# The first two dense units on x transposed by the host, the norm put into weights and results, and h made meanwhile

## The chip, the cores and the metric

The kernel runs on one core of a Trainium2 chip. The metric is device time in microseconds; the time before is 746.34 us, the median of three runs (745.83 to 747.23). Names of engines: PE is TensorE, DVE is VectorE, ACT is ScalarE, POOL is GpSimd, SP is SyncE, which issues nearly all DMAs here.

## What is computed

One decoder block on x, 256 tokens by 1024 channels, fp32. What matters for the change is its start:

```python
h = rmsnorm(x, g_mix[l])
proj = h @ w_in[l]
q_d, k_d, v_d, q_s, k_s, v_s, gate_d, gate_s = split_cols(proj, IN_WIDTHS)
```

with

```python
y = x32 * lax.rsqrt(jnp.mean(x32 * x32, axis=-1, keepdims=True) + RMS_EPS)
return (y * gain.astype(jnp.float32)).astype(x.dtype)
```

So h[t, c] = x[t, c] * r[t] * g[c], with one factor r per token and one gain g per channel. Behind it come dilated attention in three groups and sliding-window attention, two branch products merged by sigmoid gates, an output product added to x, a second norm (gain g_ffn), a router and 32 experts, of which each token uses two, and a final norm.

## The kernel before

Partitions are 128 wide, so D = 1024 is NK = 8 slices of channels and T = 256 tokens are NT = 2 tiles. The dense projection is cut into units of 512 output columns (`units`, in the order q, k, v of dilated group 1, then of groups 2 and 0, then the others). A unit's weights are two loads of 1 MB (`Stream.load`, L172, on SP; the very first load is split in two). Each fp32 operand is split into an upper part rounded to fp32r and a lower part, the remainder; `three` (L354) adds three products: upper by upper, lower by upper, upper by lower. `convert` (L240) makes both parts of two slices of a unit's weights: ACT casts the upper part (L257), DVE subtracts for the lower one (L258). There are four such pairs of buffers (set_split in the trace), so a unit's four conversions wait until TensorE has left the ones before.

`unit_steps` (L452) runs a unit in two passes of half its columns, four steps of two slices each, and `evac` (L370) takes a result out of PSUM. For q and k units the weights are stationary and h transposed (`hT_hi`, `hT_lo`, set_hT in the trace) moves, 256 columns an instruction; for v units hT is stationary and the weights move, 512 columns. Results go to two PSUM banks in turn (`acc`, L348). Four more banks (`quad`) serve the attention later.

At the start x is loaded with tokens on partitions (L148, L150). ACT and DVE each square half of a tile and sum it (L298, L299), a square root and a reciprocal give r (L285, L286), and `diag` is the identity times r (L307). A product of a slice of x with diag (`turn`, L310) then transposes it and puts r on it at once. The gain, brought to columns by a small transposing product (L303), goes on as the slice is read out of PSUM: ACT makes hT_hi (L319), DVE hT_lo (L320). Between them the first unit's weights are converted.

The order on each engine is made by a scheduler from the program's order and its dependences; `pin` keeps an instruction in the program's order. After the attention the tiles of finished stages are handed to a ring (`release`, L678), into which SP loads the expert weights (`prefetch`, L687), 2 MB a piece, 96 pieces.

Of the kernel before, what the change touches and what calls it, by code (L numbers as in the profile page):

```python
# [17 lines left out]
P = 128  # L18
T = 256
# [65 lines left out]
def tile_hybrid_block(  # L85
    ctx: ExitStack,
    tc: tile.TileContext,
    x, g_mix, w_in, w_kvs, sinks, w_br_dil, w_br_swa, w_out, g_ffn, w_group, b_group,
# [54 lines left out]
    xt = lay(4, "x", 0, [P, NT, D])  # L143
    cs = sb.tile([P, C_SMALL], F32, tag="cs", name="cs")
    ident = cs[:, C_ID:C_ID + P]
    grow = sb.tile([8, P], F32, tag="ct1", name="grow")
    frow = sb.tile([8, P], F32, tag="ct0", name="frow")
    SP.dma_start(xt[:, 0, :], x[0:P])  # L148
    A.dma_start(ident, c_small[:, C_ID:C_ID + P])
    SP.dma_start(xt[:, 1, :], x[P:T])  # L150
    A.dma_start(grow, g_mix[0].rearrange("(k p) -> k p", p=P))
# [13 lines left out]
    class Stream:  # L165
# [6 lines left out]
        def load(self):  # L172
# [41 lines left out]
    SP.dma_start(cs[:, P:], c_small[:, P:])  # L214
    SP.dma_start(frow, g_ffn[0].rearrange("(k c) -> k c", c=P))
# [24 lines left out]
    def convert(order=lambda i: i):  # L240
# [6 lines left out]
        while stream.n <= n:  # L247
# [9 lines left out]
        order(A.copy(w[:, 0, :, :ncol], r))  # L257
        order(V.tensor_tensor(  # L258
            out=w[:, 1, :, :ncol], in0=r, in1=w[:, 0, :, :ncol].bitcast(F32), op=ALU.subtract))
# [54 lines left out]
    for k in range(7):  # L314
        turn(k)
# [136 lines left out]
    def unit_steps(u):  # L452
# [5 lines left out]
        for half in range(npass):  # L458
            acc.n += 1
            o = acc()  # L460
            for kp in range(nkp):
# [26 lines left out]
                if kp == nkp - 1:  # L488
                    evac(un, half, o)
# [705 lines left out]
```

## Time and profile before

| | |
|---|---|
| time, median of three runs | 746.34 us (745.83 to 747.23) |
| the profiled execution, its own time | 747.22 us |
| its span | 745.3 us |
| TensorE busy | 627.6 us, 84% of the span |
| DVE, ACT, POOL busy | 295.3, 224.7 and 2.1 us |
| share of the chain that ended last | DMA 47%, PE 27%, ACT 5%, DVE 5% |
| expert weights on that chain | 36% and 11% of the span |

The share of busy time is a mean over stages with different limits. The chain is followed back from the last instruction to what released it each time, so it tells which engine or transfer was late in each stage; the busy times of a stretch tell how full an engine is there.

### The profile page before, as it was taken

What the parts mean: (1) busy time and instruction counts of PE and PEld (TensorE: products, weight loads), DVE (VectorE), ACT (ScalarE), POOL (GpSimd) and SP (SyncE); (2) the same over time, 40 slices, a digit from 0 to 9 for tenths busy, and PEclk for the clock granted to TensorE, in tenths of its full rate; (3) what the DMA queues carried; (4) which work ended last, traced back from release to release, by engine and by line L of the source; (5) the groups of instructions that cost most, each with busy time, mean ns of one, the idle gap of its engine ahead of it and who ended that gap; (6) DMA issues with size and microseconds to landing.
All of it is one profiled execution on the core that took longest, in us unless ns stands there. A gap on an engine that the chain in (4) does not pass through costs nothing.

```text
span 745.3 us, 14687 instructions
## 1 busy us (share of the span) xinstructions
PE 627.6 (84%) x6416; PEld 462.6 (62%) x6416; DVE 295.3 (40%) x753; ACT 224.7 (30%) x450; POOL 2.1 (0%) x10
## 2 busy tenths in 40 slices
PE   9999999999999999999887767776877677668773
PEld 8999988888998998655555434443533353334341
DVE  6554767985788566432222111211211121111003
ACT  6444566775788443301111001000100010000004
POOL 0000000000000000000000000000000000000000
PEclk9999999999999999999999878997878997997796
DMA  8746446337537978999999999999999999999992
GB/s 324 271 186 226 142 142 226 115 114 239 214 114 306 377 284 309 368 430 425 426 426 428 425 426 426 426 427 425 429 424 430 423 427 428 426 426 427 426 394 99
DMA packets 25940, 249.86 MB, mean 335 GB/s; under 512 B 5120, under 2 KB 6544, under 8 KB 8336
## 3 DMA queue, kind: packets, MB, share of 16 engines
q1 hardware_dynamic: 25712, 248.81, 82.1%
q8 instruction: 52, 0.85, 0.5%
q14 instruction: 16, 0.13, 0.0%
q10 hardware_dynamic: 160, 0.07, 0.0%
HBM read 247.82 MB, written 1.05 MB: 334 GB/s over the span
## 4 chain that ended last, share of the span: by engine, by line
DMA 47%; PE 27%; ACT 5%; DVE 5%; issue 1%; SPq 0%; DVEq 0%
DMA ew<-in_w_e_gu_dram 36%; PE acc L132 12%; DMA ew<-in_w_e_down_dram 11%; PE gu L132 5%; PE quad L132 2%; PE ga L132 2%; PE dn L132 2%; DVE set_split L258 2%; ACT set_probs L514 1%; DVE set_probs L525 1%; PE dpv L132 1%; PE dtp L594 1%; ACT set_split L257 1%; DVE set_qs L410 1%; DVE set_probs L512 1%
## 5 line engine op out<-in xcount | busy, mean ns | idle before, releaser
L132 PE MATMUL gu<-ew,xes 128*32 128x256 f32 x2048 | 152.2, 431 | 44.3 <-DMA ew<-in_w_e_gu_dram 44.2
L132 PE MATMUL acc<-set_hT,set_split 128*128 128x256 f32 x1200 | 151.6, 282 | 0.8 <-DVE set_qa L410 0.8
L132 PEld LDWEIGHTS acc<-set_hT,set_split 128*128 128x128 f32 x1200 | 142.5, 189 | 2.5 <-DVE set_qa L410 1.0
L132 PEld LDWEIGHTS gu<-ew,xes 128*32 128x32 f32 x2048 | 67.4, 120 | 106.3 <-DMA ew<-in_w_e_gu_dram 56.7
L258 DVE TENSOR_TENSOR set_split<-set_raw,set_split 128x1024 fp32r<-128x1024 f32 (+1 forms) x84 | 100.2, 1198 | 33.6 <-ACT set_split L257 31.2
L257 ACT CAST set_split<-set_raw 128x1024 fp32r<-128x1024 f32 (+1 forms) x84 | 86.3, 1028 | 41.8 <-PE acc L132 41.0
L966 DVE TENSOR_TENSOR set_raw<-set_raw,gu 128x128 f32<-128x128 f32 x32 | 9.2, 287 | 201.9 <-ACT set_raw L963 201.9
L963 ACT ACTIVATE set_raw<-gu 128x128 f32<-128x128 f32 x32 | 8.9, 277 | 230.3 <-PE gu L132 230.3
L132 PE MATMUL dn<-ew,set_raw 128*32 128x256 f32 x1024 | 71.7, 423 | 7.1 <-DMA ew<-in_w_e_down_dram 6.6
L132 PEld LDWEIGHTS dn<-ew,set_raw 128*32 128x32 f32 x1024 | 34.0, 119 | 30.8 <-issue 6.5
L132 PE MATMUL ga<-set_raw 128*128 128x128 f32 x256 | 39.5, 318 | 5.0 <-DVE set_raw L979 4.2
L992 ACT ACTIVATE y_hi<-dn,gsl 128x256 fp32r<-128x256 f32 x32 | 15.1, 473 | 91.0 <-PE dn L132 91.0
L132 PEld LDWEIGHTS ga<-set_raw 128*128 128x128 f32 x256 | 36.1, 226 | 8.9 <-DVE set_raw L979 7.0
L994 DVE SCALAR_TENSOR_TENSOR y_lo<-dn,gsl,y_hi 128x256 fp32r<-128x256 f32 x32 | 15.4, 480 | 53.5 <-ACT y_hi L992 53.5
L132 PE MATMUL acc<-set_split,set_hT 128*128 128x512 f32 x144 | 34.1, 394 | 0.3 <-DVE set_ks L420 0.2
L891 ACT ACTIVATE xes<-ga,fcol 128x128 f32<-128x128 f32 x32 | 11.6, 367 | 69.5 <-DVE xes L893 69.5
L933 DVE TENSOR_SCALAR set_raw<-cs,pos 128x128 f32<-128x128 f32 x64 | 17.8, 282 | 37.0 <-PE ct L132 37.0
L132 PE MATMUL quad<-y_hi,cts 32*128 32x256 f32 x256 | 23.7, 349 | 8.5 <-ACT y_hi L992 8.5
L132 PEld LDWEIGHTS acc<-set_split,set_hT 128*128 128x128 f32 x144 | 26.7, 188 | 6.6 <-DVE set_split L258 0.6
L132 PE MATMUL quad<-y_lo,cts 32*128 32x256 f32 x256 | 21.9, 347 | 7.7 <-DVE y_lo L994 6.5
L138 PE MATMUL atp<-cs,set_raw 128*128 128x128 f32 x32 | 11.5, 360 | 19.0 <-DVE set_raw L966 18.2
L138 PEld LDWEIGHTS atp<-cs,set_raw 128*128 128x128 f32 x32 | 4.7, 148 | 36.3 <-DVE set_raw L966 33.8
(205 smaller groups left out, 644.7 us busy)
## 6 DMA issues: line engine op xcount, KB each, us to landing
ew<-in_w_e_gu_dram SPq DMA_DIRECT2D x62, 2048.0 KB, 39.1
ew<-in_w_e_down_dram SPq DMA_DIRECT2D x31, 2048.0 KB, 39.1
set_raw<-in_w_in_dram SPq DMA_DIRECT2D x29, 1024.0 KB, 5.0
set_raw<-in_w_br_swa_dram SPq DMA_DIRECT2D x4, 1024.0 KB, 5.0
set_raw<-in_w_out_dram SPq DMA_DIRECT2D x4, 1024.0 KB, 6.2
ew<-in_w_e_gu_dram SPq DMA_DIRECT2D x4, 1024.0 KB, 33.1
set_raw<-in_w_br_dil_dram SPq DMA_DIRECT2D x2, 1024.0 KB, 4.9
set_x<-in_x_dram SPq DMA_DIRECT2D x2, 512.0 KB, 4.7
```

Source lines behind the costliest of these rows:

```text
L132: i = PE.matmul(o, lhsT, rhs, start=start, stop=stop, skip_group_check=True)
L138: i = PE.transpose(o, src, ident)
L257: order(A.copy(w[:, 0, :, :ncol], r))
L258: order(V.tensor_tensor(out=w[:, 1, :, :ncol], in0=r, in1=w[:, 0, :, :ncol].bitcast(F32), op=ALU.subtract))
L410: V.scalar_tensor_tensor(out=lo, in0=sv, scalar=cs[own, j:j + 1], in1=hi.bitcast(F32), op0=ALU.mult, op1=ALU.subtract)
L512: V.tensor_tensor_reduce(out=v, in0=s, in1=dist, scale=float(scale), scalar=init, op0=ALU.add, op1=ALU.min, accum_out=nm[:, i:i + 1])
L891: A.activation(dst, src, AF.Copy, scale=col)
L933: eq = V.tensor_scalar(dd[:, t, :].rearrange("p (g s) -> p g s", g=REP), cs[:, C_CNT:C_CNT + CAP].unsqueeze(1).to_broadcast([P, REP, CAP]) ...
L963: A.activation(ac, gu[:, 0:P], AF.Silu)
L966: V.tensor_tensor(out=ac, in0=ac, in1=gu[:, P:2 * P], op=ALU.mult)
L992: A.activation(y_hi, dn[:, 0:256], AF.Copy, scale=gsl)
L994: V.scalar_tensor_tensor(out=y_lo, in0=dn[:, 0:256], scalar=gsl, in1=y_hi.bitcast(F32), op0=ALU.mult, op1=ALU.subtract)
```

## The change

The host gives x transposed (`xT`: channels on partitions, slice by slice) beside x, and both gains as one small array of columns (`gcols`, on ACT's queue). The kernel loads the first four slices of xT, then the first half-piece of weights, then the other four slices, then the rest as before. The table of constants comes in one load.

For the first two units (q and k of group 1) the moving operand is x itself, `xT_hi` cast by ACT and `xT_lo` subtracted by POOL. Their weights get the gain as they are converted, in instructions of one slice each: ACT scales by the gain's column, DVE multiplies by it and subtracts. Their results stay in the four quad banks (`put_off`) until r is there, and get r as they are read out (`rbc`, r on all partitions, one column per token).

r comes from squares of xT (half on DVE, half on POOL), added by POOL, reduced over slices by DVE (`hsum`), summed over partitions by a product with a matrix of ones, then a square root on ACT and a reciprocal on DVE (`scale_rows`). h for the other units is made in `normal`, four times for two slices: POOL multiplies xT by rbc, ACT multiplies by the gain's columns and casts hT_hi, POOL subtracts for hT_lo. The sum of squares by ACT and DVE on tokens, diag, the transposing products and both small transposes of gains are gone.

```diff
-    xt = lay(4, "x", 0, [P, NT, D])
+    xt = lay(4, "x", 0, [P, NK, T])
     cs = sb.tile([P, C_SMALL], F32, tag="cs", name="cs")
     ident = cs[:, C_ID:C_ID + P]
-    grow = sb.tile([8, P], F32, tag="ct1", name="grow")
-    frow = sb.tile([8, P], F32, tag="ct0", name="frow")
-    SP.dma_start(xt[:, 0, :], x[0:P])
-    A.dma_start(ident, c_small[:, C_ID:C_ID + P])
-    SP.dma_start(xt[:, 1, :], x[P:T])
-    A.dma_start(grow, g_mix[0].rearrange("(k p) -> k p", p=P))
+    gcols = sb.tile([P, 2 * NK], F32, tag="gcols", name="gcols")
+    gcol, fcol = gcols[:, 0:NK], gcols[:, NK:]
+    A.dma_start(gcols, gains_in)
+    SP.dma_start(xt[:, 0:4, :], xT[:, 0:4, :])
...
                 SP.dma_start(t[:, j:j + step, :ncol], src[:, j:j + step, :])
+                if self.n == 0 and j == 0:
+                    SP.dma_start(xt[:, 4:, :], xT[:, 4:, :])
             self.tiles[self.n] = (t, s)
...
         stream.load()
-    SP.dma_start(cs[:, P:], c_small[:, P:])
-    SP.dma_start(frow, g_ffn[0].rearrange("(k c) -> k c", c=P))
+    SP.dma_start(cs, c_small)
...
         r = raw[:, 2 * half:2 * half + nk, :ncol]
-        order(A.copy(w[:, 0, :, :ncol], r))
-        order(V.tensor_tensor(
-            out=w[:, 1, :, :ncol], in0=r, in1=w[:, 0, :, :ncol].bitcast(F32), op=ALU.subtract))
+        if u < 2:
+            for j in range(nk):
+                col = gcol[:, 2 * kp + j:2 * kp + j + 1]
+                order(A.activation(w[:, 0, j, :], r[:, j, :], AF.Copy, scale=col))
+                order(V.scalar_tensor_tensor(out=w[:, 1, j, :], in0=r[:, j, :], scalar=col,
+                                             in1=w[:, 0, j, :].bitcast(F32), op0=ALU.mult, op1=ALU.subtract))
+        else:
+            order(A.copy(w[:, 0, :, :ncol], r))
+            order(V.tensor_tensor(
+                out=w[:, 1, :, :ncol], in0=r, in1=w[:, 0, :, :ncol].bitcast(F32), op=ALU.subtract))
         wtiles[(u, kp)] = w
...
-    ht = lay(4, "x", 2048, [P, NT, D])
-    ssq = sm("ssq", [P, 2, 2])
-    rs0 = sm("rs0", [P, 2])
-    diag = sb.tile([P, 1024], F32, tag="PT", name="diag")
+    G = nc.gpsimd
+    sq = lay(4, "x", 2048, [P, NK, T])
     hT_hi = lay(0, "hT", 0, [P, NK, T], F32R)
     hT_lo = lay(0, "hT", 2048, [P, NK, T], F32R)
+    xT_hi = lay(1, "xT", 0, [P, NK, T], F32R)
+    xT_lo = lay(1, "xT", 2048, [P, NK, T], F32R)
+    rbc = sb.tile([P, T], F32, tag="yh", name="rbc")
     pin = tc.keep_in_program_order
-    gcol = sm("gcol", [P, 8])
-    fcol = sm("fcol", [P, NK])
-    for t in range(NT):
-        pin(A.activation(ht[:, t, 0:512], xt[:, t, 0:512], AF.Square, accum_out=ssq[:, t, 0:1]))
-        pin(V.tensor_tensor_reduce(out=ht[:, t, 512:D], in0=xt[:, t, 512:D], in1=xt[:, t, 512:D], scale=1.0,
-                                   scalar=0.0, op0=ALU.mult, op1=ALU.add, accum_out=ssq[:, t, 1:2]))
-        if t == 1:
-            gps = bank("A1", [P, 512], "gps")
-            PE.transpose(gps[:, 0:8], grow, ident[0:8, 0:8])
-            pin(V.tensor_copy(gcol, gps[:, 0:8]))
-        pin(V.tensor_tensor(out=ssq[:, t, 0:1], in0=ssq[:, t, 0:1], in1=ssq[:, t, 1:2], op=ALU.add))
-        rstd_of(rs0[:, t:t + 1], ssq[:, t, 0:1])
-        pin(V.tensor_scalar(diag[:, t * P:(t + 1) * P], ident, rs0[:, t:t + 1], None, op0=ALU.mult))
-    hps = [bank(b, [P, 512], f"hps{b}")[:, 0:T] for b in ("T", "V", "A0")] + [quad[k][:, 0:T] for k in range(4)]
-    def turn(k):
-        for t in range(NT):
-            mm(hps[k][:, t * P:(t + 1) * P], xt[:, t, k * P:(k + 1) * P], diag[:, t * P:(t + 1) * P], True, True)
-    for k in range(7):
-        turn(k)
+    pin(V.tensor_tensor(out=sq[:, 0:4, :], in0=xt[:, 0:4, :], in1=xt[:, 0:4, :], op=ALU.mult))
     for kq in range(4):
+        if kq % 2 == 0:
+            for k0 in ((0, 2) if kq == 0 else (4,)):
+                k = slice(k0, 4 if kq == 0 and k0 else k0 + (2 if kq == 0 else 4))
+                pin(A.copy(xT_hi[:, k, :], xt[:, k, :]))
+        k = slice(2 * kq, 2 * kq + 2)
+        pin(G.tensor_tensor(out=xT_lo[:, k, :], in0=xt[:, k, :], in1=xT_hi[:, k, :].bitcast(F32), op=ALU.subtract))
         convert(pin)
-        for k in (2 * kq, 2 * kq + 1):
-            pin(A.activation(hT_hi[:, k, :], hps[k], AF.Copy, scale=gcol[:, k:k + 1]))
-            pin(V.scalar_tensor_tensor(
-                out=hT_lo[:, k, :], in0=hps[k], scalar=gcol[:, k:k + 1],
-                in1=hT_hi[:, k, :].bitcast(F32), op0=ALU.mult, op1=ALU.subtract))
-            if k == 0:
-                hps.append(bank("T", [P, 512], "hps7")[:, 0:T])
-                turn(7)
-    fps = bank("T", [P, 512], "fps")
-    PE.transpose(fps[:, 0:8], frow, ident[0:8, 0:8])
-    V.tensor_copy(fcol, fps[:, 0:8])
+    pin(G.tensor_tensor(out=sq[:, 4:, :], in0=xt[:, 4:, :], in1=xt[:, 4:, :], op=ALU.mult))
+    pin(G.tensor_tensor(out=sq[:, 0:4, :], in0=sq[:, 0:4, :], in1=sq[:, 4:, :], op=ALU.add))
+    hsum = sb.tile([P, T], F32, tag="yl", name="hsum")
+    def scale_rows():
+        pin(V.tensor_reduce(hsum, sq[:, 0:4, :].rearrange("p k t -> p t k"), axis=AX.X, op=ALU.add))
+        hs = bank("T", [P, 512], "hs")[:, 0:T]
+        i = PE.matmul(hs, warm[:, 0:1].to_broadcast([P, P]), hsum, start=True, stop=True, skip_group_check=True)
+        pin(A.activation(rbc, hs, AF.Sqrt, scale=1.0 / D, bias=eps))
+        pin(V.reciprocal(rbc, rbc))
+    def normal(kq):
+        k = slice(2 * kq, 2 * kq + 2)
+        G.tensor_tensor(out=sq[:, k, :], in0=xt[:, k, :], in1=rbc.unsqueeze(1).to_broadcast([P, 2, T]), op=ALU.mult)
+        for i in (2 * kq, 2 * kq + 1):
+            A.activation(sq[:, i, :], sq[:, i, :], AF.Copy, scale=gcol[:, i:i + 1])
+        A.copy(hT_hi[:, k, :], sq[:, k, :])
+        G.tensor_tensor(out=hT_lo[:, k, :], in0=sq[:, k, :], in1=hT_hi[:, k, :].bitcast(F32), op=ALU.subtract)
...
                 if kind == "qd" and arg:
-                    V.tensor_scalar(qk[arg][:, 0, c, :], src, cs[:, C_QD + c:C_QD + c + 1], None, op0=ALU.mult)
+                    q, sc = qk[arg][:, 0, c, :], cs[:, C_QD + c:C_QD + c + 1]
+                    if un is units[0]:
+                        V.scalar_tensor_tensor(out=q, in0=src, scalar=sc, in1=rbc, op0=ALU.mult, op1=ALU.mult)
+                    else:
+                        V.tensor_scalar(q, src, sc, None, op0=ALU.mult)
                     continue
...
         elif kind == "kd":
-            A.copy(qk[arg][:, 1, 2 * half:2 * half + 2, :], ov)
+            ks = qk[arg][:, 1, 2 * half:2 * half + 2, :]
+            if un is units[1]:
+                V.tensor_tensor(out=ks, in0=ov, in1=rbc.unsqueeze(1).to_broadcast([P, 2, T]), op=ALU.mult)
+            else:
+                A.copy(ks, ov)
         elif kind == "vd" and arg == 0:
...
             acc.n += 1
-            o = acc()
+            o = quad[2 * u + half] if u < 2 else acc()
             for kp in range(nkp):
...
                     else:
-                        b_hi, b_lo = hT_hi, hT_lo
+                        b_hi, b_lo = (xT_hi, xT_lo) if u < 2 else (hT_hi, hT_lo)
                     for cc in range(2):
...
                 if kp == nkp - 1:
-                    evac(un, half, o)
+                    if u < 2:
+                        put_off.append(lambda half=half, o=o: evac(un, half, o))
+                    else:
+                        evac(un, half, o)
                 if half == npass - 1:
...
-    for _ in steps_of(("qd", "kd", "vd")):
+    first = steps_of(("qd", "kd", "vd"))
+    for i in range(24):
+        next(first)
+        if i == 6:
+            scale_rows()
+        if 8 <= i < 16 and i % 2 == 0:
+            normal(i // 2 - 4)
+        if i >= 18 and put_off:
+            put_off.pop(0)()
+    for _ in first:
         pass
...
     a["x"] = a["x"].reshape(n // 4, 4, d).transpose(1, 0, 2).reshape(1, n, d)
+    a["xT"] = a["x"][0].T.reshape(NK, P, n).transpose(1, 0, 2)
+    a["gains"] = np.concatenate([a[g][0].reshape(NK, P).T for g in ("g_mix", "g_ffn")], axis=1)
     w = a["w_in"][0]
```

What stands on the engines' queues. Names are those of the program; `set_split` are the converted weights, `set_raw` the loaded ones, `set_x` holds x and the squares, `set_xT` the two parts of x, `set_hT` those of h. The lines of the changed kernel have its own numbers.

POOL, from the start to the first instruction that was there before as well; before:

```order
L154 MEMSET warm 128x1
L155 MEMSET warm 128x1
L898 ISA
L898 TENSOR_SCALAR set_raw_87<-cs,pos,rs_194 128x32 x4
L1029 TENSOR_LOAD overi
```

and now:

```order
L152 MEMSET warm 128x1
L153 MEMSET warm 128x1
L311 ISA
L311 TENSOR_TENSOR set_xT<-set_x,set_xT 128x512 x4
L313 TENSOR_TENSOR set_x<-set_x 128x1024
L314 TENSOR_TENSOR set_x<-set_x 128x1024
L328 TENSOR_TENSOR set_x<-set_x,rbc 128x512 x4
L332 TENSOR_TENSOR set_hT<-set_x,set_hT 128x512 x4
L922 TENSOR_SCALAR set_raw_84<-cs,pos,rs_153 128x32 x4
```

Fourteen instructions have come to POOL, ahead of the four of the first gather (L898, now L922).

ACT, from the first unit's weights to the third unit's; before:

```order
L319 ACTIVATE set_hT<-hpsA_135,gcol 128x256
L319 ACTIVATE set_hT<-quad_61,gcol 128x256
L257 CAST set_split_167<-set_raw_90 128x1024
L319 ACTIVATE set_hT<-quad_62,gcol 128x256
L319 ACTIVATE set_hT<-quad_63,gcol 128x256
L257 CAST set_split_167<-set_raw_90 128x1024
L319 ACTIVATE set_hT<-quad_64,gcol 128x256
L319 ACTIVATE set_hT<-hps_155,gcol 128x256
L257 CAST set_split_150<-set_raw_87 128x1024 x2
L257 CAST set_split_167<-set_raw_90 128x1024 x2
L423 COPY set_qk<-acc_311 128x512
L257 CAST set_split_150<-set_raw_87 128x1024 x2
```

and now:

```order
L259 ACTIVATE set_split_129<-set_raw_88,gcols 128x512 x4
L322 ACTIVATE rbc<-hs,warm 128x256
L330 ACTIVATE set_x<-set_x,gcols 128x256 x3
L331 CAST set_hT<-set_x 128x512
L330 ACTIVATE set_x<-set_x,gcols 128x256 x2
L331 CAST set_hT<-set_x 128x512
L330 ACTIVATE set_x<-set_x,gcols 128x256 x2
L331 CAST set_hT<-set_x 128x512
L263 CAST set_split_116<-set_raw_84 128x1024 x2
L330 ACTIVATE set_x<-set_x,gcols 128x256
L331 CAST set_hT<-set_x 128x512
L263 CAST set_split_129<-set_raw_88 128x1024 x2
```

h stood between the first unit's weights; now it stands behind those of the first two units, and the third unit's first two casts (L263) behind three quarters of it.

DVE, around the reduction of the squares (L319, `hsum`); before there was none, and here stood:

```order
L258 TENSOR_TENSOR set_split_167<-set_raw_90,set_split_167 128x1024
L320 SCALAR_TENSOR_TENSOR set_hT<-quad_64,gcol,set_hT 128x256
L320 SCALAR_TENSOR_TENSOR set_hT<-hps_155,gcol,set_hT 128x256
L258 TENSOR_TENSOR set_split_150<-set_raw_87,set_split_150 128x1024
L397 TENSOR_SCALAR set_qk<-acc_199,cs 128x256 x2
```

and now:

```order
L304 TENSOR_TENSOR set_x<-set_x 128x1024
L260 SCALAR_TENSOR_TENSOR set_split_116<-set_raw_84,gcols,set_split_116 128x512 x4
L260 SCALAR_TENSOR_TENSOR set_split_129<-set_raw_88,gcols,set_split_129 128x512 x4
L260 SCALAR_TENSOR_TENSOR set_split_116<-set_raw_84,gcols,set_split_116 128x512 x4
L260 SCALAR_TENSOR_TENSOR set_split_129<-set_raw_88,gcols,set_split_129 128x512 x2
L319 TENSOR_REDUCE hsum<-set_x 128x256
L544 TENSOR_SCALAR nsink<-sink 128x16
L260 SCALAR_TENSOR_TENSOR set_split_129<-set_raw_88,gcols,set_split_129 128x512 x2
L323 RECIPROCAL rbc<-rbc 128x256
L403 SCALAR_TENSOR_TENSOR set_qk<-quad_61,cs,rbc 128x256 x2
```

The reduction stands behind fourteen of the sixteen weight instructions of the first two units, two more stand between it and the reciprocal, and the reading out of the first unit stands behind both. On TensorE the product with ones stands behind the first unit's 96 products and 20 of the second's.

## Rows read from the trace of the kernel before

**Rows 1.** Chain that ended last, in order of time (start us, us, what).

```profile
356.57 1.43 PE gu L132 x22
...
358.54 39.15 DMA ew<-in_w_e_gu_dram
397.75 40.67 DMA ew<-in_w_e_gu_dram
```

**Rows 2.** Busy us by stretch: length, engines with instructions, granted clock, DMA share, GB/s.

```profile
0.00:10.00 10.00, 8.20 (x38) 6.78 (x39) 3.80 (x13) 5.39 (x13) 0.31 (x6) 1.00 0.79 295
10.00:20.00 10.00, 10.00 (x86) 9.62 (x84) 8.97 (x15) 6.55 (x12) 0.00 (x0) 1.00 0.84 311
...
44.00:100.00 56.00, 55.24 (x433) 53.00 (x432) 33.32 (x38) 28.83 (x37) 0.00 (x0) 1.00 0.50 170
...
300.00:350.00 50.00, 48.49 (x614) 29.44 (x613) 17.08 (x77) 8.49 (x26) 0.00 (x0) 0.97 0.98 407
...
400.00:450.00 50.00, 35.36 (x412) 20.89 (x408) 9.02 (x33) 4.00 (x11) 0.00 (x0) 0.82 1.01 426
```

**Rows 3.** Timeline of TensorE in the first three units (start us, us).

```profile
10.27 0.48 PE L132 MATMUL acc<-set_hT,set_split 128*128 128x256 f32 x2
...
11.22 8.77 PE L132 MATMUL acc<-set_hT,set_split 128*128 128x256 f32 x74
...
20.07 13.42 PE L132 MATMUL acc<-set_hT,set_split 128*128 128x256 f32 x116
33.32 11.15 PE L132 MATMUL acc<-set_split,set_hT 128*128 128x512 f32 x48
```

**Rows 4.** Timeline of ACT: its first instruction on x.

```profile
5.02 0.63 ACT L298 ACTIVATE set_x<-set_x 128x512 f32<-128x512 f32 x1 [1.50 <-DMA set_x<-in_x_dram]
```

**Rows 5.** Timeline of SP's queue, then what two of these issues waited for.

```profile
7.81 0.33 SPq L222 DMA_DIRECT2D set_probs<-c_big_dram  x1
9.10 0.33 SPq L224 DMA_DIRECT2D sink<-in_sinks_dram  x1
11.64 0.38 SPq L229 DMA_DIRECT2D wr<-in_w_group_dram  x1
14.07 0.37 SPq L230 DMA_DIRECT2D wr<-in_w_router_dram  x1
16.59 0.37 SPq L229 DMA_DIRECT2D wr<-in_w_group_dram  x1
...
SPq L224 <- DMA set_raw<-in_w_in_dram: 1.0, 1, 1.0
SPq L222 <- DMA set_raw<-in_w_in_dram: 0.8, 1, 0.8
```

**Rows 6.** Groups of instructions by line and form: count, busy us, mean ns of one.

```profile
L257 ACT CAST set_split<-set_raw 128x1024 fp32r<-128x1024 f32 x80 | 83.8, 1049 | 38.4 <-PE acc L132 37.7 <-ACT set_qa L418 0.3 <-ACT set_yd L610 0.2
L257 ACT CAST set_split<-set_raw 128x512 fp32r<-128x512 f32 x4 | 2.5, 620 | 3.4 <-PE acc L132 3.4
L298 ACT ACTIVATE set_x<-set_x 128x512 f32<-128x512 f32 x2 | 1.3, 630 | 1.5 <-DMA set_x<-in_x_dram 1.5
L319 ACT ACTIVATE set_hT<-quad,gcol 128x256 fp32r<-128x256 f32 x4 | 1.8, 488 | 0.0
L258 DVE TENSOR_TENSOR set_split<-set_raw,set_split 128x1024 fp32r<-128x1024 f32 x80 | 97.4, 1224 | 29.4 <-ACT set_split L257 27.0
L258 DVE TENSOR_TENSOR set_split<-set_raw,set_split 128x512 fp32r<-128x512 f32 x4 | 2.8, 693 | 4.3 <-ACT set_split L257 4.3
L132 PE MATMUL spun<-set_probs 128*128 128x256 f32 x12 | 5.0, 597 | 1.2 <-DVE set_probs L160 1.2
```

**Rows 7.** The same view: POOL's only tensor work, and small DVE instructions.

```profile
L898 POOL TENSOR_SCALAR set_raw<-cs,pos,rs 128x32 f32<-128x32 f32 x4 | 1.8, 472 | 296.3 <-ACT junk L717 296.3
L523 DVE RECIPROCAL den<-den 128x4 f32<-128x4 f32 x8 | 1.4, 175 | 0.2
L523 DVE RECIPROCAL den<-den 128x2 f32<-128x2 f32 x8 | 1.3, 162 | 1.6 <-ACT set_probs L514 1.6
L761 DVE TENSOR_SCALAR set_raw<-cs,f 128x32 f32<-128x32 f32 x2 | 0.5, 242 | 0.1
```

More of the change, by code (lines that the diff above doesn't have):

```diff
@@ L87, in tile_hybrid_block @@
     tc: tile.TileContext,
-    x, g_mix, w_in, w_kvs, sinks, w_br_dil, w_br_swa, w_out, g_ffn, w_group, b_group,
+    x, xT, gains_in, w_in, w_kvs, sinks, w_br_dil, w_br_swa, w_out, w_group, b_group,
     w_router, b_router, w_e_gu, w_e_down, g_final, c_small, c_big, out,
@@ L357, in three @@
         mm(o, a_hi, b_lo, False, stop)
-    freed = []
+    freed, put_off = [], []
     flip = [0]
@@ L1141, in tile_hybrid_block @@
     general(*tiles)
-_INS = ["x", "g_mix", "w_in", "w_kvs", "sinks", "w_br_dil", "w_br_swa", "w_out", "g_ffn", "w_group", "b_group",
+_INS = ["x", "xT", "gains", "w_in", "w_kvs", "sinks", "w_br_dil", "w_br_swa", "w_out", "w_group", "b_group",
         "w_router", "b_router", "w_e_gu", "w_e_down", "g_final"]
```

## The prediction

> **What bounds the kernel now.** I read the chain that ended last first, then the busy time by stage, then the first 45 us of TensorE's timeline, then the transfers and the single durations. In the last half the expert weights bound it: from 358.54 us on the chain is one DMA of expert weights after another [rows 1]. Just ahead of that it runs through TensorE [rows 1], which is 97% busy from 300 to 350 us while the DMA is at 0.98 [rows 2]. That DMA stream refills tiles as the earlier stages let go of them, so it is neither earlier nor later than they are. From 10 to 20 us TensorE is busy all the time and from 44 to 100 us 99%, at the full granted clock of 1.00 [rows 2]. I therefore take it that a microsecond won or lost in the first three dense units goes through to the end one for one.
>
> In that front TensorE starts on acc at 10.27, is gapless from 11.22, and begins the third unit at 33.32 [rows 3]. 116 matmuls of 256 columns take 13.42 us, 0.1157 us each; 48 of 512 columns take 11.15, 0.232 each; so the third unit ends at 33.32 + 11.15 = 44.47 [rows 3]. **44.47 is the mark**: what the change makes of it is what it makes of the time.
>
> **What is removed.** The squares, the two diag multiplications, the sixteen transposing products and eight hT_hi/hT_lo pairs leave the front. What this can give: x is there at 5.02 [rows 4]. SP's issues that wait for the weight pieces show them landing about 7.8, 9.1, 11.6, 14.1 and 16.6 us, 1.3 us for 512 KB [rows 5]. The changed queue puts the first half-piece of weights second, so it lands at 6.5, and the second half of x at 7.8; the rest is unchanged. A scaled 128x512 ACT instruction costs 0.63 [rows 6], so TensorE begins at about 7.1. The next half-piece comes at 9.1, its scaled form at 9.7; TensorE has used up its first 24 matmuls (2.8 us) by then. From 9.7 the other 168 take 19.4 us, and the one product for the sum of squares some 0.5 (an estimate; the fp32 warm-up's rows have 597 ns [rows 6]): units one and two could end at 29.6 instead of 33.3. If the third followed at once, the mark would be 40.8, **3.7 us earlier**. That is the ceiling of the gain.
>
> ACT's sixteen scaled instructions at 0.63 replace eight casts at 1.05, 1.7 us more; DVE's sixteen of 128x512 at 0.69 replace eight at 1.22, 1.3 us more [rows 6]. The landings leave both room, so I cost this at nothing. The smaller loads on ACT's queue and the whole constant table in one piece change a few KB: nothing.
>
> **What is added: h, on a path through GpSimd.** Every product of the third unit needs h, and GpSimd's queue now holds, in this order, four 128x512 lower halves of x, two 128x1024 instructions for the sum of squares, four 128x512 multiplications and four 128x512 lower halves of h. GpSimd's price is not in this trace: its only tensor rows are four 128x32 ones at 472 ns, against 242 for a TENSOR_SCALAR of the same size on DVE, 1.95 times as long [rows 7]. *Lower bound*: GpSimd's fixed part (472 less 32 columns at DVE's 1.04 ns, 0.44 us) plus 512 columns at DVE's rate, 0.97 us. *Upper bound*: the row scaled by columns, 7.5 us, which is absurd, since the row is nearly all fixed part. I take twice DVE's duration, a = 1.39 us for 512 columns and b = 2.45 for 1024. The Trainium skill (GPSIMD Engine Reference, Performance versus the Vector engine) gives 4497 ns for a tensor_tensor of 2048 fp32 columns, an estimate of 1.12 for 512; by it the four multiplications below would take 1.1 us less and the undisturbed sum would be -2.0. No run here shows it yet.
>
> The path, if GpSimd and DVE do not disturb one another: ACT scales two weight pieces and casts the second half of x, 9.1 + 2 x 0.63 + 1.05 = 11.4. GpSimd's two remaining lower halves, the squares and the addition, 2a + 2b = 7.7, end at 19.1. The reduction stands on DVE behind fourteen of the sixteen weight instructions, whose pieces land up to 16.6 and whose tiles unit one must release: about 19.8, so the addition is just hidden. Reduction 1.2 (as a 1024-column instruction) gives 21.0; product 0.5 and square root 0.5 give 22.0. The reciprocal goes by (175 - 162)/2 = 6.5 ns a column [rows 7], 1.8 us for 256; with two weight instructions ahead of it on DVE, 24.4. GpSimd's four multiplications, 4a = 5.6, give 30.0. Now **ACT's queue** counts: the third unit's weight casts stand behind the scaling and casting of h. Scaling 0.49 and cast 0.62 give 31.1; two weight casts 33.2; the last quarter of h 34.3; two more casts 36.4; DVE's lower half of the last, 37.6. TensorE still has some 26 matmuls of 512 columns then, 6.0 us: **43.6**, against 44.47. So undisturbed the change is worth only -0.9 us; 2.8 of the 3.7 go into the path of h. Each 0.1 us on a costs nearly 1 us, since 6a + 2b stand on this path.
>
> **The wait that is added.** GpSimd's instructions up to the addition lie beside ten DVE instructions that read two tiles in SBUF, as they do themselves. No row shows such a pair: the four GpSimd rows stand beside DVE work that reads PSUM or a few columns. Bounds: nothing, or each waits while the other reads. For the second, DVE reads 0.53 of its 0.69 us (slope and fixed part of the 512 and 1024 rows [rows 6]), 10 x 0.53 = 5.3; some of this fits into GpSimd's four fixed parts, 4 x 0.44 = 1.8. The addition ends at 11.4 + 7.7 + 5.3 - 1.8 = 22.6 and the reduction begins 2.8 us late. Behind it are queued DVE's last two weight instructions and, on TensorE, the product that stands after 116 matmuls (about 20.4 us): TensorE waits there with 76 matmuls of unit two behind it. In the third unit DVE's four lower halves of the weights meet GpSimd's four of h; one such wait on the path, 1.0. Together -0.9 + 2.8 + 1.0 = **+2.9**. I take this end because GpSimd's row was measured with nothing in its way, and because DVE's two-tile instruction already takes a column each 1.04 ns without a pause (531 ns for 512 more columns). The Trainium skill (SBUF — State Buffer, Who interferes with whom) says that a DVE instruction with two SBUF inputs and a GpSimd instruction that reads SBUF block each other, the later one fully. That speaks against the change; by it, taken literally, the sum is that of rival 3, and no run here shows it yet.
>
> **The rivals.**
> 1. *They run freely, GpSimd at twice DVE's price*: -0.9 us. For it: ACT, DVE and TensorE read SBUF beside one another through the front at their usual durations.
> 2. *Freely, and GpSimd near its floor*: a = 0.97 takes 4 x 0.42 = 1.7 us off the four multiplications, -2.6 us, about 743.7. This ends on the other side: faster. It decides from a of about 1.2 downward.
> 3. *Whole instructions exclude each other*: ten times 0.69 with nothing hidden in fixed parts, 6.9 instead of 3.5 (less the 0.7 that is hidden), and more meetings in the third unit: +6 to +7, some 752.8.
> 4. TensorE's stalls could cost clock: between 400 and 450 us it is 71% busy and has 0.82 granted [rows 2]. In the front it had 1.00 throughout, and gaps of one or two microseconds are all that I expect; I leave it to the tail.
>
> **How the numbers follow.** The profiled run took 747.22 us, 0.88 above the median of 746.34; I set the change against both alike and give the result on the median: 746.34 + 2.9 = **749.2**. Chances: the forecast (+1 to +5) 0.40, of it 0.36 slower by over 0.2% (1.5 us, about what a measurement of this kernel can tell from no change); rival 1 0.25, of it 0.20 within 0.2% and 0.05 faster; rival 2 0.22, all faster; rival 3 with the tail 0.13, slower. So faster 0.27, same 0.24, slower 0.49. The range reaches from rival 2 to rival 3, 743.8 to 752.6.
>
> **What would show each step.** Right: the first matmul on xT near 7 us; GpSimd's 128x512 instructions at 1.4 us or more up to 20 us and shorter in 24 to 30 us, when DVE reads PSUM; DVE's weight instructions over 0.69 while GpSimd runs; TensorE waiting at the ones product for the reduction; the third unit ending after 46 us. Wrong: the third unit ending before 44, DVE at 0.69 throughout, or a below 1.2. It would also be wrong if the first expert transfers moved by another amount than the mark: then the one-for-one step fails.

## The result

The changed kernel takes 755.8 us, the median of four runs (755.3 to 756.36): 1.0118 times the kernel before, 95% interval 1.0097 to 1.0139, about 9 us slower. The profiled execution took 756.36 us, its span is 754.6. The forecast had the sign right, and that GpSimd and DVE would wait for one another; it charged that wait to the wrong engine and had a third of the size.

TensorE in the first units, as in [rows 3] (timeline: start us, us, engine, line, what; in brackets the idle time before and who ended it):

```profile
6.99 0.58 PE L132 MATMUL quad<-set_xT,set_split 128*128 128x256 f32 x2 [0.33 <-ACT set_split L259]
...
9.53 5.89 PE L132 MATMUL quad<-set_xT,set_split 128*128 128x256 f32 x47 [0.95 <-DVE set_split L260]
...
17.89 0.62 PE L132 MATMUL quad<-set_xT,set_split 128*128 128x256 f32 x3 [0.96 <-DVE set_split L260]
20.64 7.86 PE L132 MATMUL quad<-set_xT,set_split 128*128 128x256 f32 x51 [2.13 <-DVE set_split L260]
28.45 0.70 PE L321 MATMUL hs<-hsum,warm 128*128 128x256 f32 x2
28.80 9.45 PE L132 MATMUL quad<-set_xT,set_split 128*128 128x256 f32 x76
39.05 0.98 PE L132 MATMUL acc<-set_split,set_hT 128*128 128x512 f32 x3 [0.79 <-ACT set_split L263]
40.56 1.66 PE L132 MATMUL acc<-set_split,set_hT 128*128 128x512 f32 x6 [0.54 <-DVE set_split L264]
42.80 1.89 PE L132 MATMUL acc<-set_split,set_hT 128*128 128x512 f32 x7 [0.57 <-DVE set_split L264]
45.04 7.57 PE L132 MATMUL acc<-set_split,set_hT 128*128 128x512 f32 x32 [0.35 <-DVE set_split L264]
52.44 23.20 PE L132 MATMUL acc<-set_hT,set_split 128*128 128x256 f32 x192
75.47 4.72 PE L132 MATMUL acc<-set_split,set_hT 128*128 128x512 f32 x20
```

TensorE starts 3.3 us earlier than before, and then waits again and again for DVE's lower halves. The mark, the end of the third unit, is 45.04 + 7.57 = 52.61 where it was 44.47: +8.1 us. Another 1.3 are lost behind it: the 192 matmuls of units four and five take 23.20 where the kernel before has 21.95, so its second v unit began at 66.10 and this one's at 75.47, +9.4. The row of the kernel before:

```profile
44.31 21.95 PE L132 MATMUL acc<-set_hT,set_split 128*128 128x256 f32 x192
```

Busy time by stretch, as in [rows 2] (length, PE, PEld, DVE, ACT, POOL, granted clock, DMA share, GB/s):

```profile
10.00:20.00 10.00, 7.38 (x58) 6.77 (x56) 8.57 (x6) 7.02 (x11) 7.95 (x4) 1.00 0.86 318
44.00:100.00 56.00, 55.22 (x383) 51.34 (x383) 31.87 (x34) 26.39 (x31) 0.00 (x0) 1.00 0.53 188
...
400.00:450.00 50.00, 35.44 (x480) 20.75 (x476) 10.08 (x36) 4.47 (x12) 0.00 (x0) 0.94 1.00 426
```

TensorE, busy all of 10 to 20 us before, is busy for 7.38 of it, with GpSimd at 7.95; from 44 us on it is as full as before, and the tail again waits for expert weights. What is lost is lost in the front.

Who was late shows in DVE's timeline, first weights to third unit:

```profile
6.97 2.51 DVE L260 SCALAR_TENSOR_TENSOR set_split<-set_raw,gcols,set_split 128x512 fp32r<-128x512 f32 x2 [0.85 <-ACT set_split L259]
10.38 1.41 DVE L260 SCALAR_TENSOR_TENSOR set_split<-set_raw,gcols,set_split 128x512 fp32r<-128x512 f32 x2 [0.90 <-ACT set_split L259]
12.84 10.39 DVE L260 SCALAR_TENSOR_TENSOR set_split<-set_raw,gcols,set_split 128x512 fp32r<-128x512 f32 x8 [1.05 <-ACT set_split L259]
25.07 1.42 DVE L260 SCALAR_TENSOR_TENSOR set_split<-set_raw,gcols,set_split 128x512 fp32r<-128x512 f32 x2 [1.83 <-ACT set_split L259]
26.40 2.00 DVE L319 TENSOR_REDUCE hsum<-set_x 128x256 f32<-128x1024 f32 x1
...
29.76 1.75 DVE L323 RECIPROCAL rbc<-rbc 128x256 f32<-128x256 f32 x1
...
39.03 3.71 DVE L264 TENSOR_TENSOR set_split<-set_raw,set_split 128x1024 fp32r<-128x1024 f32 x2 [4.51 <-ACT set_split L263]
...
43.26 2.85 DVE L264 TENSOR_TENSOR set_split<-set_raw,set_split 128x1024 fp32r<-128x1024 f32 x2
```

and beside it GpSimd's:

```profile
5.60 3.33 POOL L311 TENSOR_TENSOR set_xT<-set_x,set_xT 128x512 fp32r<-128x512 f32 x2 [4.74 <-ACT set_xT L309]
11.97 3.01 POOL L311 TENSOR_TENSOR set_xT<-set_x,set_xT 128x512 fp32r<-128x512 f32 x2 [3.04 <-ACT set_xT L309]
14.94 2.35 POOL L313 TENSOR_TENSOR set_x<-set_x 128x1024 f32<-128x1024 f32 x1
17.36 2.67 POOL L314 TENSOR_TENSOR set_x<-set_x 128x1024 f32<-128x1024 f32 x1
31.65 5.28 POOL L328 TENSOR_TENSOR set_x<-set_x,rbc 128x512 f32<-128x512 f32 x4 [11.62 <-DVE rbc L323]
36.89 7.01 POOL L332 TENSOR_TENSOR set_hT<-set_x,set_hT 128x512 fp32r<-128x512 f32 x4
```

At 10.38 and 25.07, with GpSimd idle, two of DVE's weight instructions take 1.41 and 1.42 us. At 12.84 eight take 10.39, and GpSimd's lower halves, squares and addition fill this stretch up to 17.36 + 2.67 = 20.03. Two of the eight by themselves:

```profile
15.46 2.38 DVE L260 SCALAR_TENSOR_TENSOR set_split<-set_raw,gcols,set_split 128x512 fp32r<-128x512 f32 x1
17.76 2.83 DVE L260 SCALAR_TENSOR_TENSOR set_split<-set_raw,gcols,set_split 128x512 fp32r<-128x512 f32 x1
```

They end at 17.84 and 20.59, each 0.55 us behind the end of one of GpSimd's long instructions (17.29 and 20.03). So the two engines take turns, one instruction each. A turn cost DVE most of a long GpSimd instruction, 1.6 and 2.1 us here. GpSimd loses less: its squares and addition took 2.35 and 2.67 us, where e1 below has 1.90 and 2.41.

ACT's queue closes a loop (timeline of ACT):

```profile
12.09 5.14 ACT L259 ACTIVATE set_split<-set_raw,gcols 128x512 fp32r<-128x512 f32 x8 [0.19 <-DMA set_raw<-in_w_in_dram]
24.31 2.81 ACT L259 ACTIVATE set_split<-set_raw,gcols 128x512 fp32r<-128x512 f32 x4 [7.09 <-PE quad L132]
...
37.96 1.99 ACT L263 CAST set_split<-set_raw 128x1024 fp32r<-128x1024 f32 x2
```

DVE late makes TensorE late, TensorE lets go of the weight buffers late, ACT waits 7.09 us for them, and DVE's thirteenth and fourteenth weight instructions wait for ACT. The reduction stands behind these two, so it begins at 26.40, though the sum it reads stood at 20.03.

### The profile page after: what moved, and what is told of

It reads as the page before. It is cut to its first block, busy times and chain, and to the rows that moved or that the text cites. A ratio compares the mean times of both kernels' runs of the same rounds, so it can differ in the third digit from the quotient of the medians.

```text
span 754.6 us, 14642 instructions
## 1 busy us (share of the span) xinstructions
PE 619.8 (82%) x6384; PEld 457.1 (61%) x6384; DVE 304.9 (40%) x746; ACT 228.7 (30%) x458; POOL 25.7 (3%) x24
## 4 chain that ended last, share of the span: by engine, by line
DMA 50%; PE 25%; DVE 5%; ACT 3%; issue 1%; SPq 0%; DVEq 0%; ACTq 0%
DMA ew<-in_w_e_gu_dram 31%; DMA ew<-in_w_e_down_dram 19%; PE acc L132 14%; PE gu L132 3%; PE quad L132 2%; DVE set_split L264 1%; PE dn L132 1%; PE ga L132 1%; DVE set_qs L418 1%; ACT set_probs L529 1%; PE spv L132 1%; PE stp L571 1%; PE dtp L609 1%; ACT set_qs L417 1%; PE dpv L132 0%
## 5 line engine op out<-in xcount | busy, mean ns | idle before, releaser
L132 PE MATMUL gu<-ew,xes 128*32 128x256 f32 x2048 | 148.6, 422 | 53.9 <-DMA ew<-in_w_e_gu_dram 53.8
L132 PE MATMUL acc<-set_hT,set_split 128*128 128x256 f32 x1008 | 132.8, 287 | 0.4 <-DVE set_qa L418 0.4
L132 PEld LDWEIGHTS acc<-set_hT,set_split 128*128 128x128 f32 x1008 | 124.2, 191 | 2.1 <-DVE set_qa L418 0.6
L264 DVE TENSOR_TENSOR set_split<-set_raw,set_split 128x1024 fp32r<-128x1024 f32 (+1 forms) x76 | 92.1, 1219 | 32.0 <-ACT set_split L263 30.8
L263 ACT CAST set_split<-set_raw 128x1024 fp32r<-128x1024 f32 (+1 forms) x76 | 77.5, 1024 | 37.5 <-PE acc L132 36.5
L132 PE MATMUL ga<-set_raw 128*128 128x128 f32 x256 | 35.9, 298 | 5.0 <-DVE set_raw L1003 4.2
L132 PEld LDWEIGHTS ga<-set_raw 128*128 128x128 f32 x256 | 32.8, 208 | 8.8 <-DVE set_raw L1003 6.9
L915 ACT ACTIVATE xes<-ga,gcols 128x128 f32<-128x128 f32 x32 | 11.6, 367 | 66.3 <-DVE xes L917 66.3
L132 PE MATMUL quad<-set_xT,set_split 128*128 128x256 f32 x192 | 26.5, 298 | 4.8 <-DVE set_split L260 4.5
L132 PEld LDWEIGHTS quad<-set_xT,set_split 128*128 128x128 f32 x192 | 25.1, 203 | 6.6 <-DVE set_split L260 5.5
```

Of the source, the lines that this page charges most:

```text
L132: i = PE.matmul(o, lhsT, rhs, start=start, stop=stop, skip_group_check=True)
L264: order(V.tensor_tensor(out=w[:, 1, :, :ncol], in0=r, in1=w[:, 0, :, :ncol].bitcast(F32), op=ALU.subtract))
L915: A.activation(dst, src, AF.Copy, scale=col)
```

## The experiments

The "mark" is the end of the third unit, "units four and five" the 192 matmuls behind it, "first quarter" the 24 products of the first unit that follow its first two. T, T2, R1, R2, A and B are the theories that an expectation names.

**e0, the kernel before once more.**

> The kernel before, unchanged, profiled on the chip of the next three kernels. It settles a side question: in the changed kernel's trace the 192 matmuls of 256 columns of the fourth and fifth units took 23.20 us where the trace of before has 21.95, at the same granted clock, 1.3 of the 9.4 us. If that pace belongs to the chip or the execution, before can show either pace here, and e1 to e3 have the same as this run; if it belongs to the change, this run has 21.95 and e1 to e3, whose code is the same from there on, 23.20. The mark (end of the third unit) is expected at 44.5 in either case.

Mark 44.46, units four and five 21.95, 746.93 us. The slower pace is the change's.

**e1, DVE's second operand from PSUM.**

```diff
-                                             in1=w[:, 0, j, :].bitcast(F32), op0=ALU.mult, op1=ALU.subtract))
+                                             in1=spun, op0=ALU.mult, op1=ALU.subtract))
```

> The changed kernel, but DVE's sixteen weight instructions of the first two units take their second operand from a PSUM bank of zeros instead of the upper half in SBUF; the upper half is left out of the subtraction, all else is computed as in the changed kernel. GpSimd keeps its fourteen instructions. Theory T (DVE's instructions with two operands in SBUF and GpSimd's block each other for whole instructions, and the late DVE then holds up TensorE and the weight buffers): DVE's sixteen at 0.75 us, GpSimd's four lower halves of x at 1.30 and its squares near 2.3, the reduction near 20 instead of 26.4, the mark at 43 to 45.5 instead of 52.6, the time 7 to 9 us below the changed kernel's, 746 to 749. Rival R1 (GpSimd's own price and the long path of h): the reduction stays later than 24 and the mark later than 50, above 753. Rival R2 (no more than the clock that TensorE lost when it stood still): DVE's durations stay as they were, 1.1 in the mean, and the mark moves only as far as TensorE's stall does.

Groups of instructions in the first 50 us (count, busy us, mean ns of one, idle before), first of the changed kernel, then of e1, then two rows of e1's DVE timeline:

```profile
L260 DVE SCALAR_TENSOR_TENSOR set_split<-set_raw,gcols,set_split 128x512 fp32r<-128x512 f32 x16 | 17.1, 1126 | 4.6 <-ACT set_split L259 4.6
```

```profile
L261 DVE SCALAR_TENSOR_TENSOR set_split<-set_raw,gcols,spun 128x512 fp32r<-128x512 f32 x16 | 11.1, 743 | 4.3 <-DMA set_raw<-in_w_in_dram 3.3 <-PE quad L132 1.0
...
L312 POOL TENSOR_TENSOR set_xT<-set_x,set_xT 128x512 fp32r<-128x512 f32 x4 | 5.5, 1383 | 8.3 <-ACT set_xT L310 8.3
```

```profile
19.91 2.01 DVE L320 TENSOR_REDUCE hsum<-set_x 128x256 f32<-128x1024 f32 x1
...
32.97 4.56 DVE L265 TENSOR_TENSOR set_split<-set_raw,set_split 128x1024 fp32r<-128x1024 f32 x2 [4.91 <-ACT set_split L264]
```

In the changed kernel these sixteen took 1126 ns in the mean; here they take 743, and the reduction starts at 19.91, as T said. The mark is 46.87, missing T's 43 to 45.5, because the third unit's two instructions, left as they were, now take 4.56 us instead of 2.4. Time 751.17 us, 1.0056 (1.004 to 1.0072) times before: 4.6 below the changed kernel, not 7 to 9. R1 is out for the front, and R2 too, since DVE's durations fell; the rest of the loss was left to e7 and e4. GpSimd's lower halves of x took 1383 ns in the mean, not T's 1.30 us, since the first of them met DVE's squares and took 1.65. DVE no longer waits for ACT's upper halves either, so this run alone doesn't part that from the blocking; e10 does.

**e2, GpSimd's work on DVE.** `G = nc.vector` instead of `nc.gpsimd`.

> The changed kernel with GpSimd's fourteen instructions on DVE, all else the same: nothing is left for DVE to share with. T: every 128x512 instruction near 0.69 to 0.75 and every 128x1024 one near 1.22; up to the reduction DVE then has some 17 us of work from 6.5 us on, so the reduction starts at about 24, two us before the changed kernel's, but the sixteen weight instructions and all of h run undisturbed: mark at 46 to 49, time 748.5 to 752. R1 (the path of h is long whoever walks it): DVE has one queue where there were two, so the reduction comes after 27 and the mark after 52, 755 or more.

TensorE's timeline:

```profile
11.23 13.22 PE L132 MATMUL quad<-set_xT,set_split 128*128 128x256 f32 x108 [0.17 <-DVE set_split L260]
...
32.06 11.37 PE L132 MATMUL acc<-set_split,set_hT 128*128 128x512 f32 x48
43.27 23.20 PE L132 MATMUL acc<-set_hT,set_split 128*128 128x256 f32 x192
```

746.73 us, ratio 1.0002 (0.9987 to 1.0017). One engine doing all is 9 us better than two that block each other. The mark, 43.43, is 2.6 to 5.6 below what I expected: the reduction came at 22.48, not 24, and h found gaps between DVE's other work. It is 1.0 below the kernel before, and units four and five take 1.25 back.

**e3, squares on ACT, nothing on GpSimd.** ACT squares x as fp32r, eight products with ones replace addition and reduction, DVE makes x's lower halves and h:

```diff
+            pin(A.activation(sqr[:, k, :], xt[:, k, :], AF.Square))
...
+        for k in range(NK):
+            mm(hs, one.to_broadcast([P, P]), sqr[:, k, :], k == 0, k == NK - 1)
...
+            V.scalar_tensor_tensor(out=sq[:, i, :], in0=xt[:, i, :], scalar=gcol[:, i:i + 1], in1=rbc,
+                                   op0=ALU.mult, op1=ALU.mult)
```

> A version without GpSimd: DVE makes the lower halves of x; ACT squares x in two instructions rounded to fp32r, and eight one-pass products with ones sum over slices and partitions at once, so no addition and no reduction; DVE multiplies x by gain and r in one instruction a slice, ACT casts, DVE subtracts. T: the sum of squares stands by 16 us, r by 24, h by 33, TensorE waits for less than 1 us: mark at 41.5 to 43.5, 743 to 745.5, faster than the kernel before by 1 to 3 us. R1 (the path of h bounds in any form): mark at 44.5 or later, 746 or more.

746.13 us, 0.9989 (0.9974 to 1.0004), mark 44.73: missed. Its profile is of the slowest of its ten runs (747.58): the granted clock was 0.50 from 10 to 12 us, and the first quarter took 4.63 us, where e5 below has 3.12.

**e7, the third unit too.** e1, and the third unit's subtraction also takes the bank of zeros.

> e1 with the third unit's lower halves treated as the first two units': their second operand from the PSUM bank of zeros, so the upper half is left out of three units' subtraction. In e1 two of these instructions beside GpSimd's last ones for h took 4.56 us and the mark was 46.70. T (the same blocking in the third unit): four at 1.23 us each, GpSimd's lower halves of h at 1.26, mark 43.8 to 45.0, about 2 us below e1. R1 (the path of h): mark stays at 46.3 to 46.9.

```profile
L333 POOL TENSOR_TENSOR set_hT<-set_x,set_hT 128x512 fp32r<-128x512 f32 x4 | 5.1, 1290 | 0.3 <-ACT set_hT L332 0.3
...
L266 DVE TENSOR_TENSOR set_split<-set_raw,spun 128x1024 fp32r<-128x1024 f32 x4 | 4.7, 1215 | 0.3 <-DMA set_raw<-in_w_in_dram 0.3
```

(the groups of the first 50 us). Mark 44.45, 748.41 us, 1.0014 (1.0001 to 1.0028); 2.8 below e1. T holds here too. With GpSimd's fourteen instructions in place and no blocking at the weights, the mark is where it was before the change.

**e10, GpSimd only writes.** Each step up to the reduction is three memsets; DVE keeps both operands in SBUF.

> The changed kernel, but GpSimd only writes up to the reduction: each of its four lower halves of x is three memsets of the same 128x512, each of its two 128x1024 steps of the sum of squares three memsets; lower halves of x and the sum of squares are left out. DVE's weight instructions keep both operands in SBUF. T (the blocking is between reads): DVE's weight instructions at 0.75 us beside the memsets, reduction near 20. T2 (any access of GpSimd to SBUF holds DVE up): DVE's instructions over 1 us while the memsets run, that is up to some 14 us.

Timelines of GpSimd and of DVE:

```profile
7.31 2.97 POOL L315 MEMSET set_x<- 128x1024 f32 x3
10.23 2.97 POOL L317 MEMSET set_x<- 128x1024 f32 x3
```

```profile
6.87 1.41 DVE L260 SCALAR_TENSOR_TENSOR set_split<-set_raw,gcols,set_split 128x512 fp32r<-128x512 f32 x2 [0.95 <-ACT set_split L259]
...
10.47 1.41 DVE L260 SCALAR_TENSOR_TENSOR set_split<-set_raw,gcols,set_split 128x512 fp32r<-128x512 f32 x2 [2.18 <-ACT set_split L259]
...
20.25 2.00 DVE L322 TENSOR_REDUCE hsum<-set_x 128x256 f32<-128x1024 f32 x1
```

T, not T2: two pairs of DVE's weight instructions ran beside memsets, and each took 1.41 us, as alone. What blocks is that both read. The third unit, where GpSimd reads as in the changed kernel, keeps its loss (3.69 us for DVE's first two instructions there, 3.71 in the changed kernel; mark 46.30; 749.15 us, one run). By the Trainium skill (SBUF — State Buffer, Who interferes with whom) a DVE instruction with two SBUF inputs collides with a GpSimd instruction that reads SBUF, and not with one that only writes it: e1, e7 and e10 agree.

**e6, e4, e5: 64 bytes.** An unused tile of 64 bytes ahead of the weights, in the changed kernel (e6) and in e2 (e4); in e3 the small tile of ones made 64 bytes long (e5). Addresses are those that the program gives its tiles.

```diff
     rbc = sb.tile([P, T], F32, tag="yh", name="rbc")
+    gap = sb.tile([P, 16], F32, tag="gap", name="gap")
+    nc.gpsimd.memset(gap, 0.0)
```

> e2 (GpSimd's work on DVE) with one unused tile of 64 bytes a partition ahead of the converted weights, which moves their address by 64 bytes and does no more. Ground: e0 has 21.95 us for the 192 matmuls of units four and five on the chip where e1 and e2 have 23.20 with the same code, so the pace belongs to the change; what differs for these units is where tiles lie. Modulo 512 bytes the weights stand 64 bytes behind h in the kernel before, level with h in the changed kernel, e1 and e2, 32 behind in e3 (22.88 us). Theory A (the address sets the pace): 21.95 again in units four and five and about 22.2 in units one and two, mark 42.0, second v unit 2.5 us earlier than in e2, time 744 to 745, below before. Rival B (something else in the changed program, such as its order): 23.20 and 746.7 stay.

> e3 (ACT's squares, DVE for the rest) with its small tile of ones made 64 bytes a partition instead of 4, so that the weights stand 64 bytes behind h modulo 512 as in the kernel before. A: 192 matmuls in 21.95 instead of 22.88, mark 43.5 instead of 44.6, time 744 to 745. B: as e3, 746.1.

> The changed kernel with the unused tile of 64 bytes and nothing else, to part the two causes in its own time. A: units four and five take 21.95 instead of 23.20, so 1.3 us of the second v unit's 9.4 go; the mark moves by less than 0.7, since TensorE waits in units one and two anyway: 753.5 to 754.5. B: 755.3 to 756.

e4: units four and five in 21.95, the second v unit 1.1 earlier than in e2 (65.17 to 66.30; I had 2.5), mark 43.55, where I had expected 42.0; 745.38 us, 0.9985 (0.9972 to 0.9998). e5: 22.78, where I had expected 21.95, and mark 41.89, where I had 43.5; **744.05 us**, 0.9958 (0.9942 to 0.9973), faster than both kernels. e6: 22.78, neither A's value nor B's, and mark 51.09; 754.52 us, 1.0101 (1.0078 to 1.0123). So the pace goes with the address, but e4 and e6 agree in it and not in the pace.

e6 holds a second thing. Its mark fell by 1.5, more than the 0.7 that I gave the 64 bytes. Busy time by stretch (length, PE, PEld, DVE, ACT, POOL, granted clock, DMA share, GB/s), of the changed kernel and then of e6:

```profile
15.00:20.00 5.00, 2.38 (x16) 1.77 (x14) 5.00 (x3) 2.22 (x4) 4.92 (x2) 1.00 0.71 209
20.00:22.00 2.00, 1.36 (x7) 1.36 (x8) 2.00 (x4) 0.00 (x0) 0.04 (x1) 0.71 0.21 20
22.00:24.00 2.00, 2.00 (x11) 2.00 (x11) 1.24 (x2) 0.00 (x0) 0.00 (x0) 0.50 0.28 33
```

```profile
10.00:12.00 2.00, 2.00 (x12) 2.00 (x11) 1.41 (x2) 1.88 (x3) 0.04 (x1) 0.50 1.01 426
...
15.00:20.00 5.00, 3.43 (x27) 3.02 (x26) 5.00 (x3) 2.40 (x4) 4.91 (x2) 1.00 0.72 209
...
22.00:24.00 2.00, 2.00 (x20) 2.00 (x19) 1.65 (x3) 1.22 (x2) 0.00 (x0) 1.00 0.56 56
```

and two rows of e6's TensorE timeline:

```profile
9.42 9.04 PE L132 MATMUL quad<-set_xT,set_split 128*128 128x256 f32 x59 [0.94 <-DVE set_split L260]
20.59 6.27 PE L132 MATMUL quad<-set_xT,set_split 128*128 128x256 f32 x51 [2.13 <-DVE set_split L260]
```

From 15 to 20 us TensorE waits for DVE in both, busy for 2.38 and 3.43 of the 5 us. Once in the front its clock fell to the lower of its two levels (0.50, 1.2 GHz) for a while. In the changed kernel it fell behind this wait, with work there: 51 matmuls took 7.86 us from 20.64 on. In e6 it fell earlier, behind a wait of 0.94 us that ended at 9.42; the changed kernel has the same wait (0.95, to 9.53) and no fall behind it. In e6 the fall cost little, since DVE was later still: e6 begins its 51 matmuls at 20.59, at clock 1.00, and they took 6.27. The reduction, which stands behind these buffers, began at 26.40 in the one and at 24.87 in the other. That is read from a pair of profiles; no run was made for the clock alone.

**e8, e9: 128 and 192 bytes,** in e5.

> e5 with the converted weights 128 instead of 64 bytes behind h modulo 512. So far, by this distance, the 192 matmuls of units four and five took: level 23.20 us (changed kernel, e1, e2, e7), 32 bytes 22.88 (e3), 64 bytes 21.95 (before, e4) or 22.78 (e5, e6). If the distance alone sets the pace, all kernels of one distance agree, which e4 and e6 already deny; if it sets it together with where in its rhythm TensorE enters the unit, the pace here is one of these values again or near, 21.9 to 23.2; if it has no part, the value is that of e5, 22.78, for 128 and 192 alike. Time 743 to 745.

> The same with 192 bytes, expected as for 128: 22.78 in both if the distance has no part, other values (21.9 to 23.2) if it has. Time 743 to 745.

Units four and five: 23.20 (e8) and 22.77 (e9); 746.82 us, 0.9994 (0.9985 to 1.0004), and 745.44, 0.9977 (0.9966 to 0.9988), both above the 743 to 745 that I expected. The pace moves with the distance, and the distance isn't all. e8's profile, of its slowest run (749.01), has the clock at 0.50 from 8 to 10 us.

**e11, one warm-up product more,** in e5.

> e5, the fastest so far, with seven warm-up products instead of six. Ground: in the profiles of e3 and e8 TensorE stood idle for 1.55 and 1.28 us between the warm-up and its first product on x, and its granted clock fell to 0.50 for some 3 us, so the first unit's first quarter took 4.63 us; in e5 and e9 it idled for 1.41 and 0.40, the clock stayed at 1.00 and the quarter took 3.12 and 3.26. One more product of 0.8 us leaves less than 0.8 of idling. If the idling costs the clock: 1.00 throughout, the quarter in 3.1 to 3.3, the slowest of the runs come down, median 743.5 to 744.3. If not: as e5 or, by the half microsecond by which a late warm-up can delay the first product, up to 744.6.

Clock 1.00, first quarter 3.36, mark 42.08, units four and five 21.95, though every address is e5's; 744.31 us, 0.9966 (0.995 to 0.9982). The median doesn't tell it from e5, so that the warm-up helps isn't shown.

## Why the prediction was too small

**One for one: right.** The second v unit began 9.4 us later, the first expert load was issued at 179.2 instead of 169.4, the time rose by about 9.

**Start at 7.1: right. GpSimd's prices: right, but for the squares.** First product on x at 6.99. GpSimd took 5.28 us for four multiplications, which met no weight instruction of DVE (a = 1.32; I had 1.39), and 1.90 and 2.41 for the two of 1024 columns in e1 (I had 2.45 for both). So rival 2, GpSimd near its floor, was out. The Trainium skill's figure (GPSIMD Engine Reference, Performance versus the Vector engine), an estimate of 1.12 for 512 columns, is below the 1.32 that was measured. Reciprocal 1.75 against 1.8. The third unit's casts stood behind three quarters of h on ACT, as worked out, and began at 37.96.

**The wait added: right in kind, wrong in its victim. This step failed.** I let GpSimd lose: addition at 22.6, reduction just behind. GpSimd lost about 1 us (20.03 against 18.94 in e1). DVE lost: sixteen weight instructions at 1.126 instead of 0.743, 6.1 us in sum, where I had them at 0.69 and wrote "I cost this at nothing", since the landings leave room. From there the loss went through what the sum did not follow: TensorE waiting for lower halves long before the ones product, the buffers, ACT's 7.09, DVE again. The reduction came 3.8 us later than my 22.6, and by the pair above (e6 and the changed kernel) some 1.5 of that was the clock, rival 4, which I had left to the tail.

**Terms mis-sized.** Reduction 2.00, not 1.2, and 1.99 in e2 with GpSimd silent, so no wait is in it: the price of another 1024-column instruction, which reads its slices in a row, didn't carry over. The third unit's wait: 1.0 predicted, 2.4 of mark between e1 and e7; in the changed kernel DVE's last lower half ends 3.2 us behind ACT's last cast, where 1.2 and this 1.0 were priced. That 6a + 2b stand on the path didn't fit my own sum, in which 2a + 2b were hidden behind DVE and only 4a counted.

**Sum.** Predicted mark 44.47 + 2.9 = 47.4, measured 52.6, 5.2 more: 3.8 up to the reduction; 0.9 from there to the end of the third unit's fourth lower half (18.8 predicted, 26.40 to 46.11 = 19.7 measured); 0.5 in its last matmuls, 6.5 us instead of 6.0. Behind the mark 1.3 of pace, which no step of mine had. Rival 3, whole instructions excluding each other, was the nearest: the exclusion is what the runs show. But it too charged the wait to GpSimd, and at 752.8 it was short by the loop, the clock and the pace.

**In times:** e7 with no blocking at the weights stands 1.6 us above before, with units four and five 1.3 us slower. e1 adds 2.8 for the third unit, the changed kernel 4.6 more for the first two units with their loop and clock.

Some of what the change was to give can be had: without GpSimd, with ACT squaring and with the 64 bytes, e5 is at 0.9958 of before (2.7 us), against a ceiling of 3.7. Without the 64 bytes (e3) the gain isn't clear of none.

## What to carry to other kernels

Before giving GpSimd work beside DVE, list the DVE instructions of that stretch that take both operands from SBUF. Each can wait for a whole GpSimd instruction that reads SBUF, and the price is to be followed round the loop DVE, TensorE, buffers, ACT, not only along GpSimd's own path. One DVE doing all of it can be faster, as in e2. An operand in PSUM takes the collision away (e1, e7). That the landings leave an engine room is no reason to cost its instructions at nothing, when the other engine reads in the same stretch.

## What the runs showed of the hardware

- GpSimd's instructions that read SBUF and DVE's that take two operands from it exclude each other by whole instructions. DVE's 128x512 ones took 2.38 and 2.83 us instead of 0.74, each ending 0.55 us behind the end of one of GpSimd's; two 1024-column ones took 4.56 us instead of 2.4 in e1. Writes by GpSimd don't hold DVE up (e10), and with an operand in PSUM DVE isn't held up (e1, e7).
- The pace of fp32r matmuls of 256 columns goes with where weights and moving operand lie: 192 of them, at granted clock 1.00, took 23.20 us in all five profiles with the two level modulo 512 bytes and in that with 128 between them, 22.88 with 32, 22.77 with 192, and 21.95 or 22.78 with 64. Here is the pair that leaves it open, e5 and e11, with the same addresses:

```profile
41.73 22.78 PE L132 MATMUL acc<-set_hT,set_split 128*128 128x256 f32 x192
```

```profile
41.92 21.95 PE L132 MATMUL acc<-set_hT,set_split 128*128 128x256 f32 x192
```

What else decides, perhaps the rhythm in which TensorE enters a unit, wasn't found.
- TensorE's clock fell to 0.50 behind waits of 1.55 us (e3), 1.28 (e8) and 0.94 (e6), and stayed at 1.00 behind 1.41 (e5), 1.43 (e4) and 1.57 (e7). The length of the wait alone doesn't tell which.
